# Block sums loaded one tile at a time, the last attention head's trip read ahead of other transfers, and three output tiles inside the steps

## The chip, the cores and the metric

The kernel runs on one core of a Trainium2 chip. The metric is the time of one execution on the device, in microseconds (us). A core has a matrix engine (TensorE, PE in the profile), a vector engine (VectorE, DVE), a scalar engine (ScalarE, ACT), a general engine (GpSimd, POOL) and a sync engine (SyncE, SP) that here does nothing but issue transfers (DMAs). ACT and POOL issue transfers too. Each engine works through its own list of instructions in order, and stops at an instruction whose operands aren't ready. So whatever stands behind a waiting transfer in SP's list waits with it, though it may itself be ready.

## The reference

One transformer block on 512 tokens and 16 meta tokens, model width 1024, in f32: half a feed-forward network (FFN), a mixer, and half of a second FFN.

```
h = h + 0.5 * swiglu(rmsnorm(h, ffn1_norm), ffn1_w_gate, ffn1_w_up, ffn1_w_down)     # width 2816
u = rmsnorm(h, mix_norm)
rq, rk, rv, rg, aq, ak, av, iq, ik, iw, g_ret, g_att = split(u @ w_in)
yr = (silu(rg) * retention(rq, rk, rv)) @ w_ret_out          # 4 heads, keys 256 wide, values 512 wide
ya = sparse_attention(aq, ak, av, iq, ik, iw) @ w_att_out    # 8 heads of 128; the keys of a query
                                                             # are picked by an indexer
h = h + (sigmoid(g_ret) * yr + sigmoid(g_att) * ya) @ w_mix_out
h = h + 0.5 * swiglu(rmsnorm(h, ffn2_norm), ffn2_w_gate, ffn2_w_up, ffn2_w_down)
y = rmsnorm(h, final_norm)[:, 16:]
```

## The kernel before

**Products.** An f32 product is made of three matmuls. Each operand is split into a high part and a low remainder, and `mm3` issues high by high, high by low, low by high for every 128 rows k of the contraction (line 170). For a weight tile, ACT copies `raw` into `whi` (the high part) and DVE subtracts to get `wlo` (the low one). Of the three matmuls of a k, the third needs `wlo`.

**Steps.** The mixer is written as a list of steps, run by `steps_through`: each has a tile of weights (loaded into `raw` by SP, four steps ahead), its split (two steps ahead), and its matmuls. In steps marked "dma" DVE is spared (`in_two_by_dma`): ACT writes the high part into `whi` (line 310) and its negative into `wlo` (line 311), and POOL issues a transfer that adds `raw` onto `wlo` (line 312). That transfer has to land before the step's third matmul. PE, ACT and DVE run in the order in which the program is written. SP and POOL are ordered by a scheduler, except for transfers that are kept in program order (`tc.keep_in_program_order`).

**Block sums.** The second FFN uses sums and differences of blocks of its weights. `block_sums(8)` forms those of `w_down` early, beside the last 37 retention steps: for each of 8 indices k, four tiles `wq` (256 KB each) are loaded by SP (line 1578), DVE makes four sums in place (line 1590), and four stores put them into DRAM as `wx` (line 1582). `with_block` hooks one piece of this to the end of each step. Most of those 37 steps are products of retention: gates, queries, keys, and the four output products of each head, `outputs(p)`. Those of the last head, `outputs(3)`, have the PE tile `psro`; the step after them is a gate (`psgate`). All five are "dma" steps.

**Attention.** For head h, `half_scores(h)` makes the probabilities in tokens by keys, and `trip(h)` writes them to DRAM (`pt`, issued by POOL, line 2279; even and odd heads have a `pt` of their own). `fetch(h)` reads them back the other way round (`turned`, SP, line 2292). `come_back` splits them into `pth` (ACT) and `ptl` (DVE). `weigh_v(h)` multiplies them with the values (`psao`), and its result is split into `vo` high (ACT) and low (DVE): the parts `ao_parts[h]`. A gate made between (`gate_product`, `psga`) is written to DRAM as `gd` (line 2356). The product with `w_att_out` needs all 8 heads' parts, one k for each head. Two of its eight output tiles (`psat`) are begun inside the steps, by `out_step`, with k = 0 to 6; the last head's `weigh_v` comes after them, and `out_tile_ends` adds k = 7.

Of the kernel before, what the change touches and what calls it, by code (L numbers as in the profile page):

```python
# [18 lines left out]
P = 128  # L19
D = 1024  # L20
KD = D // P
S = 512
# [11 lines left out]
AH = 8  # L34
# [47 lines left out]
def kernel(ctx: ExitStack, tc: tile.TileContext, x, meta, g1, wg1, wu1, wd1, gm,  # L82
                      w_in, w_ro, w_ao, w_mo, g2, wg2, wu2, wd2, gf, rope, decay, causal, out):
    nc = tc.nc
# [42 lines left out]
    w_at = [8]  # L127


    raw_room, raw_at = [], [0]  # L130

    def four_rooms():

# [3 lines left out]
    def load_w(src, nk, n):  # L137
        if raw_room:
            both = nk * n > 1024
            at = (raw_at[0] + (both and raw_at[0] % 2)) % 4  # L140
            raw_at[0] = at + 1 + both
            raw = raw_room[at // 2][:, at % 2 * 1024 :]
        else:
            raw = wpool.tile([P, 2048], F32, tag="raw", name="raw", bufs=2)
        v = raw[:, : nk * n].rearrange("p (k c) -> p k c", k=nk)
        nc.sync.dma_start(v, src.rearrange("(k p) c -> p k c", p=P))
        return v

    def split_w(v, eng=nc.vector):
# [208 lines left out]
    class Sevens:  # L358
# [97 lines left out]
        def catch_up(self):  # L456

            now, self.behind = self.behind, []
            for do in now:
                do()  # L460
# [1103 lines left out]
    def block_room(tag):  # L1564
        if tag == "R":
            return cpool.tile([P, T], F32, tag="R", name="wq", bufs=2)[:, :S]
        if tag == "ssum2":
            return cpool.tile([P, T], F32, tag="ssum2", name="wq")[:, :S]
        return bp.tile([P, S], F32, tag=tag, name="wq")

    def block_sums(n):

        def bring(k):

            ts = []
            for tag, (half, cs) in zip(("R", "R", "ssum2", "caus"), BLOCKS):
                ts.append(block_room(tag))
                tc.keep_in_program_order(nc.sync.dma_start(ts[-1], wrows[half][:, k, cs]))
            return ts

        def store(i, k):
            tc.keep_in_program_order(nc.sync.dma_start(wx[i, :, k, :], ts[BLOCK_SUMS[i][0]]))

        ts = bring(0)
        yield
        for k in range(n):
            for i, (to, x, y, op) in enumerate(BLOCK_SUMS):
                if i:
                    store(i - 1, k)
                nc.vector.tensor_tensor(ts[to], ts[x], ts[y], op)  # L1590
                if k % 2 == 0 or i != 2:
                    yield
            store(3, k)
            if k + 1 < n:
                ts = bring(k + 1)
                yield

    accs, vrs = ExitStack(), ExitStack()
    acc_r = []
# [33 lines left out]
    if True:  # L1633
# [438 lines left out]
        def with_block(step):  # L2072

            def run(w, lower):
                step[2](w, lower)
                next(block_steps, None)
            return (*step[:2], run, *step[3:])
# [41 lines left out]
        def attention_steps(kind, what, tiles_):  # L2119

            def step(i, t):
                return (t[0], lambda: in_parts(t[1]()), lambda w, lower: at_step[kind](*what, i, w, lower), 0)
            return [step(i, t) for i, t in enumerate(tiles_)]
# [7 lines left out]
        for h in range(AH):  # L2131
# [5 lines left out]
            else:  # L2137
                more += gate_for("scored gate", h)
            more += gate_for("weighed gate", h)
        more += attention_steps("out", (), tiles(w_ao, 0, 2))  # L2140
        steps[-37:] = [with_block(step) for step in steps[-37:]]
        last_step = steps[-1]
        steps[-1] = (*last_step[:2], lambda w, lower: (last_step[2](w, lower), at_step.update(begun=True)), *last_step[3:])
        steps += more
# [48 lines left out]


    vrs.close()
    ao_cols, psats = Cols(w_ao, 0, KD), []
    def out_tile_ends(w, ps):

        mm3([(ps, slice(0, S))], [part[:, KD - 1 :] for part in w], lambda k: ao_parts[KD - 1], 1, False, True, True)
        return ps  # L2200

    with pool("ao") as ao:
        vo = [ao.tile([P, AH, S], F32R, tag=f"vo{i}", name="vo") for i in range(2)]
        ao_parts = [(vo[0][:, c, :], vo[1][:, c, :]) for c in range(AH)]
        with pool("at") as at:
# [139 lines left out]
            def gate_product(kind, c, w, place):  # L2345

                ps = place()
                mm3([(ps, REAL)], w, xs, KD)

                def taken():  # L2350
                    t = at.tile([P, S], F32, tag="gate", name="gate", bufs=2)
                    tanh_half(t, ps)
                    if kind == "gr":
                        pending.append(lambda: gate_twice(c, t))
                    else:
                        nc.sync.dma_start(gd[KD + c], t)
                return taken

            def wide_place():
# [106 lines left out]

            def out_step(i, w, lower):

                catch_up()
                ps = sm_tile("psat") if i else mm_tile("psat")[:, :S]  # L2470
                mm3([(ps, slice(0, S))], w, lambda k: ao_parts[k], KD - 1, onto=True)
                psats.append((w, ps))
                lower()
                lower()
                for low in come_back(((0, 1), (2, 3))[i]):
                    low()

# [4 lines left out]
            with tc.manual_schedule(engines=BUSY):  # L2482
                for _ in pipe:
                    pass
                weigh_v(AH - 1)()()
            ao_cols.next_at(2)

        mgs = ExitStack()
        mgp = mgs.enter_context(pool("mgp", 1, side="right"))
        mg = []  # L2490
        with pool("ou") as ou:
            tp.update(pool=ou, bufs=3)
            for c in range(2):
                t = ou.tile([P, S], F32, tag="gate", name="gate", bufs=1)
                nc.scalar.dma_start(t, gd[c])
                gate_acc(c, t)
            psats = [out_tile_ends(*a) for a in psats]
            for c in range(KD):
                if c < len(psats):
                    ps = psats[c]  # L2500
                else:
                    w = ao_cols.next()
                    ps = sm_tile("psat")
                    mm3([(ps, slice(0, S))], w, lambda k: ao_parts[k], KD)
                t = ou.tile([P, S], F32, tag="sa", name="sa", bufs=3)
                nc.scalar.dma_start(t, gd[KD + c])
                nc.vector.scalar_tensor_tensor(t, t, 1.0, ps, ALU.add, ALU.mult)
                if c in doubled:
                    nc.vector.tensor_tensor(t, t, acc_r[c], ALU.add)
                else:  # L2510
                    nc.vector.scalar_tensor_tensor(t, t, 0.5, acc_r[c], ALU.mult, ALU.add)
                mh = mgp.tile([P, S], F32R, tag=f"mh{c}", name="mh")
                ml = mgp.tile([P, S], F32R, tag=f"ml{c}", name="ml")
                if c in doubled:
                    nc.scalar.activation(mh, t, AF.Copy, scale=0.5)
                    nc.vector.scalar_tensor_tensor(ml, t, 0.5, mh.bitcast(F32), ALU.mult, ALU.subtract)
                else:
                    split(t, mh, ml)
                mg.append((mh, ml))
# [8 lines left out]
    with pool("om") as ou:  # L2528
        tp.update(pool=ou, bufs=3)
        def to_tokens(c, hc):  # L2530
            ps = sm_tile("psht")
            for b in range(4):
                nc.tensor.transpose(ps[:, b * P : (b + 1) * P], hc[:, b * P : (b + 1) * P], ident)
            for b in range(4):
                nc.scalar.activation(hTok[b][:, c * P : (c + 1) * P], ps[:, b * P : (b + 1) * P], AF.Copy)

        cols = Cols(w_mo, 0, KD)
        pend = None
        for c in range(KD):
            hc = ou.tile([P, S], F32, tag="hc", name="hc", bufs=4)  # L2540
            nc.scalar.dma_start(hc, hd[c])
            w = cols.next()
            ps = sm_tile("psmo")
            mm3([(ps, slice(0, S))], w, lambda k: mg[k], KD)
            if pend:
                to_tokens(*pend)
            nc.vector.tensor_tensor(hc, ps, hc, ALU.add)
            h, l = new_x(c)
            if c % 4 == 0:
                s2.new_scaled()  # L2550
            xc = s2.xn[c // 4][:, c % 4, :]
            nc.scalar.activation(xc, hc, AF.Identity, scale=gains[:, 2, c : c + 1])
            split(xc, h[:, :S], l[:, :S])
            add_square(hc, ssum3, c == 0, ou, S)
            pend = (c, hc)
        last_tokens = lambda a=pend: to_tokens(*a)
        RS = slice(0, S)


        norm = rstd_steps(ssum3, S, D, R3, ou, lambda: sm_tile("psn"))  # L2560
        raw_room.clear()
        raw0 = load_w(wg2[:, 0 : 2 * P], KD, 2 * P)
        ps0 = [sm_tile("psg") for _ in range(2)]
        for i in range(2):
            w = split_w(raw0[:, :, i * P : (i + 1) * P])
            mm3([(ps0[i], RS)], w, xs, KD)
            if i == 0:
                last_tokens()
                next(norm)
        raw0 = load_w(wu2[:, 0 : 2 * P], KD, 2 * P)  # L2570
        w = split_w(raw0[:, :, :P])
        for _ in norm:
            pass
# [369 lines left out]
```

## Time and profile before

| | |
|---|---|
| median of 3 runs | 1502.78 us (1502.63 to 1506.17) |
| the profiled execution's own time | 1504.8 us |
| its span in the profile | 1503.0 us |
| mean granted clock of PE | 0.996 of full speed |
| transfers | 283.65 MB, mean 189 GB/s |
| block sums beside the steps | 32 loads, 32 sums, 32 stores of 128x512 |

The views used below: the page has the busy time of each engine. The waits list, by engine and instruction, how long an engine stood idle until what released it ("engine line waited for: us in total, times, longest us"). A timeline has one row for an instruction: its start in us from the span's start, its duration, the engine (PE, ACT, DVE, POOL; with a q, as SPq, the queue in which it issues transfers), line, operation, tiles, and in brackets the idle time before it with what ended it. For a transfer the duration is that of the issue, not of the move. Windows give, for a stretch of time A:B, its length, the busy time of PE, PE's weight loads, DVE, ACT and POOL with their counts, the granted clock of PE (1.00 is full speed), the transfer engines' share of time, and GB/s. The chain of waits is the path that ended last in a stretch, with start and length of each piece; there a transfer has its whole time to landing.

### The profile page before, as it was taken

To read this page: it belongs to the slowest core of one execution; us is meant where nothing else is said; L and a number is where in the kernel's file an instruction comes from. 1 tells how busy PE (TensorE), PEld (TensorE's weight loads), DVE (VectorE), ACT (ScalarE), POOL (GpSimd) and SP (SyncE) were. 2 spreads that over 40 slices of the span, in tenths; PEclk is the share of its full clock that TensorE was granted. 3 is DMA by queue.
4 is the path that set the end of the run, shared out by engine and by line. 5 is a ranking of instruction groups with operands and counts; after the bars stand their busy time and mean duration, and the time that the engine had idled before them with its cause. 6 is when DMAs were issued, how large, how long until landed. Compare 5 with 4: busy or idle time off the path is not lost.

```text
span 1503.0 us, 24593 instructions
## 1 busy us (share of the span) xinstructions
PE 1486.1 (99%) x9535; PEld 1339.2 (89%) x9535; DVE 1175.5 (78%) x1781; ACT 779.6 (52%) x1248; POOL 223.4 (15%) x311
## 2 busy tenths in 40 slices
PE   9999999999999999999999989999999999999998
PEld 8999999999888888788798878889788889999986
DVE  4999999788887767677968676778565779998878
ACT  5655555466354444544334436766445445555555
POOL 1012221001110121102010012111102003322101
PEclk9999999999999999999999999999999999999999
DMA  5259898886553455578685597676653224455693
GB/s 177 85 179 270 259 282 260 265 292 220 182 190 141 155 165 140 129 213 190 171 248 158 163 256 189 187 211 176 210 172 110 84 85 135 155 174 175 236 322 137
DMA packets 206102, 283.65 MB, mean 189 GB/s; under 512 B 10976, under 2 KB 138104, under 8 KB 205088
## 3 DMA queue, kind: packets, MB, share of 16 engines
q1 hardware_dynamic: 170992, 213.71, 43.9%
q0 software_dynamic: 31600, 62.52, 16.9%
q10 hardware_dynamic: 3392, 5.84, 1.1%
q8 instruction: 75, 1.23, 0.3%
q14 instruction: 43, 0.35, 0.1%
HBM read 212.79 MB, written 60.31 MB: 182 GB/s over the span
## 4 chain that ended last, share of the span: by engine, by line
PE 87%; DVE 5%; DMA 3%; issue 3%; ACT 1%; POOL 0%; POOLq 0%; ACTq 0%; SPq 0%; DVEq 0%
PE psqX L170 12%; PE psrg L170 6%; PE psqY L170 5%; PE psvX L1365 4%; PE psro L170 4%; PE psga L170 3%; PE psrk L170 3%; PE psu L170 3%; PE psrq L170 3%; PE psmo L170 3%; PE psqZ L170 3%; PE psaq L170 3%; PE psX L1040 2%; PE psak L170 2%; PE psat L170 2%
## 5 line engine op out<-in xcount | busy, mean ns | idle before, releaser
L305 ACT ACTIVATE whi<-raw 128x1024 fp32r<-128x1024 f32 (+2 forms) x216 | 204.1, 946 | 137.0 <-PE psqZ L170 21.2
L306 DVE TENSOR_TENSOR wlo<-raw,whi 128x1024 fp32r<-128x1024 f32 (+2 forms) x216 | 237.8, 1102 | 42.9 <-ACT whi L305 41.9
L170 PE MATMUL psqX<-th,whi 128*128 128x264 f32 (+1 forms) x432 | 123.3, 285 | 1.3 <-DVE g L552 0.9
L170 PE MATMUL psqX<-tl,whi 128*128 128x264 f32 (+1 forms) x432 | 122.2, 283 | 0.0
L170 PE MATMUL psqX<-th,wlo 128*128 128x264 f32 (+1 forms) x432 | 122.2, 283 | 0.0
L305 ACT ACTIVATE whi<-wsum 128x1024 fp32r<-128x1024 f32 x72 | 76.1, 1057 | 40.2 <-issue 21.3
L306 DVE TENSOR_TENSOR wlo<-wsum,whi 128x1024 fp32r<-128x1024 f32 x72 | 86.6, 1217 | 0.7 <-ACT whi L305 0.6
L170 PEld LDWEIGHTS psqX<-th,whi 128*128 128x128 f32 x432 | 82.0, 190 | 2.4 <-DVE g L552 1.1
L170 PEld LDWEIGHTS psqX<-tl,whi 128*128 128x128 f32 x432 | 82.0, 190 | 0.0
L170 PEld LDWEIGHTS psqX<-th,wlo 128*128 128x128 f32 x432 | 82.0, 190 | 0.0
L170 PE MATMUL psro<-vo,whi 128*128 128x512 f32 x256 | 81.3, 399 | 0.5 <-DVE accr L2008 0.5
L312 POOL DMA_DIRECT2D wlo<-raw x21 | 28.4, 1354 | 252.0 <-ACT wlo L311 96.2
L170 PEld LDWEIGHTS psro<-vo,whi 128*128 128x128 f32 x256 | 49.4, 193 | 11.7 <-ACT whi L310 0.9
L170 PE MATMUL psro<-vo,wlo 128*128 128x512 f32 x128 | 51.6, 403 | 4.3 <-DMA wlo<-raw 4.3
L117 ACT ACTIVATE whi<-raw 128x1024 fp32r<-128x1024 f32 (+1 forms) x31 | 31.8, 1028 | 41.5 <-PE psmo L170 21.2
L170 PE MATMUL psrg<-xh,whi 128*128 128x512 f32 x128 | 51.8, 405 | 0.0
L170 PE MATMUL psrg<-xh,wlo 128*128 128x512 f32 x128 | 50.0, 390 | 0.0
L170 PE MATMUL psrg<-xl,whi 128*128 128x512 f32 x128 | 49.9, 390 | 0.0
L2731 POOL TENSOR_TENSOR ts<-g 128x256 f32<-128x256 f32 x16 | 22.3, 1412 | 176.6 <-DVE g L563 176.6
L306 DVE TENSOR_TENSOR wlo<-w,whi 128x1024 fp32r<-128x1024 f32 x30 | 36.5, 1222 | 13.1 <-ACT whi L305 13.1
L118 DVE TENSOR_TENSOR wlo<-raw,whi 128x1024 fp32r<-128x1024 f32 (+1 forms) x31 | 36.8, 1187 | 8.2 <-ACT whi L117 8.1
L305 ACT ACTIVATE whi<-w 128x1024 fp32r<-128x1024 f32 x30 | 31.7, 1057 | 20.1 <-PE psvX L1365 10.9
(523 smaller groups left out, 4915.1 us busy)
## 6 DMA issues: line engine op xcount, KB each, us to landing
raw<-in_ffn_w_up_dram SPq DMA_DIRECT2D x22, 1024.0 KB, 5.9
raw<-in_ffn_w_gate_dram SPq DMA_DIRECT2D x21, 1024.0 KB, 6.9
raw<-in_w_in_dram SPq DMA_DIRECT2D x35, 512.0 KB, 4.7
raw<-in_ffn_w_down_dram SPq DMA_DIRECT2D x34, 512.0 KB, 4.6
raw<-in_w_in_dram SPq DMA_DIRECT2D x17, 1024.0 KB, 5.5
raw<-wx SPq DMA_DIRECT2D x32, 512.0 KB, 5.9
w<-in_w_in_dram SPq DMA_DIRECT2D x24, 512.0 KB, 6.2
wlo<-raw POOLq DMA_DIRECT2D x21, 512.0 KB, 5.7
```

Source lines behind the costliest of these rows:

```text
L117: nc.scalar.activation(hi, src, AF.Copy)
L118: eng.tensor_tensor(lo, src, hi.bitcast(F32), ALU.subtract)
L170: nc.tensor.matmul(o, a[:, k, :], b[:, sl], start=first and k == 0 and i == 0, stop=last and k == nk - 1 and i == 2, skip_group_check=onto)
L305: nc.scalar.activation(hi, src, AF.Copy)
L306: return lambda: nc.vector.tensor_tensor(lo, src, hi.bitcast(F32), ALU.subtract)
L312: return lambda: nc.gpsimd.dma_start(lo, src, accum_op=ALU.add)
L1040: nc.tensor.matmul(pss[c], a[:, k, c * P : (c + 1) * P], m[:, k, :], start=first and k == 0 and i == 0, stop=last and k == 1 and i == 2, s ...
L1365: nc.tensor.matmul(d[bank_][t], a, b[:, k, :], start=not onto and j + k + m == 0, stop=j + k == 3 and m == 2, skip_group_check=onto)
L2731: nc.gpsimd.tensor_tensor(ts[:, i], a, b, ALU.subtract)
```

## The change

Three edits. `block_sums` keeps four tiles for good; each is loaded again singly, when its sum has been stored, where four were loaded together before. It is hooked to `steps[-37:-3]`, so it ends three steps earlier. In attention, the transfers `gd` of the last two gates are issued by ACT instead of SP, and the `w_att_out` tiles that are loaded behind the steps are kept in program order (`raw_pinned`), which puts them behind the last head's `turned`. And three output tiles instead of two stand in the steps: two do k = 0 to 5, then comes the last head's `weigh_v`, then k = 6 of both, k = 7 of both, and the third tile whole.

```diff
-        nc.sync.dma_start(v, src.rearrange("(k p) c -> p k c", p=P))
+        ins = nc.sync.dma_start(v, src.rearrange("(k p) c -> p k c", p=P))
+        if raw_pinned:
+            tc.keep_in_program_order(ins)
         return v
...
-        def bring(k):
-
-            ts = []
-            for tag, (half, cs) in zip(("R", "R", "ssum2", "caus"), BLOCKS):
-                ts.append(block_room(tag))
-                tc.keep_in_program_order(nc.sync.dma_start(ts[-1], wrows[half][:, k, cs]))
-            return ts
+        ts = [block_room(tag) for tag in ("R", "R", "ssum2", "caus")]
+
+        def bring(j, k):
+            if k < n:
+                half, cs = BLOCKS[j]
+                tc.keep_in_program_order(nc.sync.dma_start(ts[j], wrows[half][:, k, cs]))
 
         def store(i, k):
-            tc.keep_in_program_order(nc.sync.dma_start(wx[i, :, k, :], ts[BLOCK_SUMS[i][0]]))
-
-        ts = bring(0)
+            if k >= 0:
+                tc.keep_in_program_order(nc.sync.dma_start(wx[i, :, k, :], ts[BLOCK_SUMS[i][0]]))
+
+        for j in range(4):
+            bring(j, 0)
         yield
         for k in range(n):
             for i, (to, x, y, op) in enumerate(BLOCK_SUMS):
-                if i:
-                    store(i - 1, k)
+                store((i - 1) % 4, k - (i == 0))
+                for j in {0: (0, 3) if k else (), 1: (), 2: (2,), 3: (1,)}[i]:
+                    bring(j, k + (i > 0))
                 nc.vector.tensor_tensor(ts[to], ts[x], ts[y], op)
-                if k % 2 == 0 or i != 2:
-                    yield
-            store(3, k)
-            if k + 1 < n:
-                ts = bring(k + 1)
                 yield
+        store(3, n - 1)
...
-        more += attention_steps("out", (), tiles(w_ao, 0, 2))
-        steps[-37:] = [with_block(step) for step in steps[-37:]]
+        more += attention_steps("out", (), tiles(w_ao, 0, 3))
+        steps[-37:-3] = [with_block(step) for step in steps[-37:-3]]
...
-    ao_cols, psats = Cols(w_ao, 0, KD), []
+    ao_cols, psats = Cols(w_ao, 3 * P, KD - 3), []
...
-                        nc.sync.dma_start(gd[KD + c], t)
+                        (nc.scalar if c >= KD - 2 else nc.sync).dma_start(gd[KD + c], t)
...
             def out_step(i, w, lower):
 
+                if i == 2:
+                    out_ = weigh_v(AH - 1)
+                    for a in psats:
+                        out_tile_goes_on(*a, KD - 2)
+                    out_()()
+                    for a in psats:
+                        out_tile_goes_on(*a, KD - 1)
+                    ps = sm_tile("psat")
+                    mm3([(ps, slice(0, S))], w, lambda k: ao_parts[k], KD)
+                    psats.append((w, ps))
+                    return
                 catch_up()
                 ps = sm_tile("psat") if i else mm_tile("psat")[:, :S]
-                mm3([(ps, slice(0, S))], w, lambda k: ao_parts[k], KD - 1, onto=True)
+                mm3([(ps, slice(0, S))], w, lambda k: ao_parts[k], KD - 2, onto=True)
                 psats.append((w, ps))
-                lower()
-                lower()
+                if i == 0:
+                    lower()
+                    lower()
                 for low in come_back(((0, 1), (2, 3))[i]):
                     low()
...
-                weigh_v(AH - 1)()()
-            ao_cols.next_at(2)
-
...
+                    raw_pinned[:] = [True]
                     w = ao_cols.next()
```

`out_tile_goes_on(w, ps, k)` takes the place of `out_tile_ends`: the three matmuls of one k onto a tile. In the changed kernel a line has a number larger by 2 (lines 170, 1578, 1582) or smaller by 1 (lines 2292, 2356).

The first place is SP's list around `outputs(3)`; the `w_ret_out` loads of 128x4x512 are the weights of that head's four products, `w_in` those of the steps behind. Before:

```order
L1582 DMA wx<-wq 128x512 x3
L1578 DMA wq<-in_ffn_w_down_dram 128x512 x4
L146 DMA raw<-in_w_ret_out_dram 128x4x512
L1582 DMA wx<-wq 128x512
L146 DMA raw<-in_w_ret_out_dram 128x4x512
L1582 DMA wx<-wq 128x512 x2
L146 DMA raw<-in_w_in_dram 128x8x128 x2
L1582 DMA wx<-wq 128x512
L1578 DMA wq<-in_ffn_w_down_dram 128x512 x4
L146 DMA raw<-in_w_in_dram 128x8x128 x2
L1582 DMA wx<-wq 128x512
```

In the changed kernel, from the same two `w_ret_out` loads on:

```order
L146 DMA raw<-in_w_ret_out_dram 128x4x512
L1580 DMA wq<-in_ffn_w_down_dram 128x512
L1584 DMA wx<-wq 128x512
L1580 DMA wq<-in_ffn_w_down_dram 128x512
L1584 DMA wx<-wq 128x512
L1580 DMA wq<-in_ffn_w_down_dram 128x512
L146 DMA raw<-in_w_ret_out_dram 128x4x512
L1580 DMA wq<-in_ffn_w_down_dram 128x512
L1584 DMA wx<-wq 128x512 x2
L146 DMA raw<-in_w_in_dram 128x8x128 x2
L1584 DMA wx<-wq 128x512 x2
L146 DMA raw<-in_w_in_dram 128x8x128 x9
```

The four last loads of `wq`, which stood together behind the first two `w_in` loads and a store, now stand singly among the stores, ahead of those two `w_in` loads; behind them only two stores are left.

The second place is SP's list at the end of attention (`pt_89` is the DRAM tile of even heads, `pt_90` that of odd ones; the last head is odd). Before:

```order
L2356 DMA gd<-gate 128x512
L2292 DMA turned<-pt_89 128x512 x4
L146 DMA raw<-in_w_att_out_dram 128x8x256
L2356 DMA gd<-gate 128x512 x2
L146 DMA raw<-in_w_att_out_dram 128x8x256
L2292 DMA turned<-pt_90 128x512 x4
L146 DMA raw<-in_w_att_out_dram 128x8x256
```

In the changed kernel:

```order
L2355 DMA gd<-gate 128x512
L2291 DMA turned<-pt_89 128x512 x4
L2291 DMA turned<-pt_90 128x512 x4
L146 DMA raw<-in_w_att_out_dram 128x8x256 x2
L146 DMA raw<-in_w_att_out_dram 128x8x128
```

Two `gd` stores and two loads of weights no longer stand between the last two heads' reads.

The third place is PE's list right behind the last head's `weigh_v`, whose last matmul is the first row; `vo_9495` and `vo_9496` (`vo_9467` and `vo_9468` in the changed kernel) hold the high and low parts of all heads, and each `psat` number is one output tile. Before:

```order
L1760 MATMUL psao_11391<-ptail_9504,vtail_9502 128x16
L170 MATMUL psat_11328<-vo_9495,whi_11166 128x512
L170 MATMUL psat_11328<-vo_9496,whi_11166 128x512
L170 MATMUL psat_11328<-vo_9495,wlo_11167 128x512
L170 MATMUL psat_11358<-vo_9495,whi_11269 128x512
L170 MATMUL psat_11358<-vo_9496,whi_11269 128x512
L170 MATMUL psat_11358<-vo_9495,wlo_11270 128x512
L170 MATMUL psat_11448<-vo_9495,whi_11444 128x512
```

In the changed kernel:

```order
L1760 MATMUL psao_11362<-ptail_9476,vtail_9474 128x16
L172 MATMUL psat_11303<-vo_9467,whi_11139 128x512
L172 MATMUL psat_11303<-vo_9468,whi_11139 128x512
L172 MATMUL psat_11303<-vo_9467,wlo_11140 128x512
L172 MATMUL psat_11332<-vo_9467,whi_11242 128x512
L172 MATMUL psat_11332<-vo_9468,whi_11242 128x512
L172 MATMUL psat_11332<-vo_9467,wlo_11243 128x512
L172 MATMUL psat_11303<-vo_9467,whi_11139 128x512
L172 MATMUL psat_11303<-vo_9468,whi_11139 128x512
L172 MATMUL psat_11303<-vo_9467,wlo_11140 128x512
L172 MATMUL psat_11332<-vo_9467,whi_11242 128x512
```

The six matmuls right behind `weigh_v` were those of k = 7, which use its result; now six of k = 6, which don't, stand between. The number of matmuls is the same.

More of the change, by code (lines that the diff above doesn't have):

```diff
@@ L127 @@
     w_at = [8]
-    raw_room, raw_at = [], [0]
+    raw_room, raw_at, raw_pinned = [], [0], []
     def four_rooms():
@@ L2195, with out_tile_goes_on @@
     vrs.close()
-    ao_cols, psats = Cols(w_ao, 0, KD), []
-    def out_tile_ends(w, ps):
-        mm3([(ps, slice(0, S))], [part[:, KD - 1 :] for part in w], lambda k: ao_parts[KD - 1], 1, False, True, True)
-        return ps
+    ao_cols, psats = Cols(w_ao, 3 * P, KD - 3), []
+    def out_tile_goes_on(w, ps, k):
+        mm3([(ps, slice(0, S))], [part[:, k:] for part in w], lambda _: ao_parts[k], 1, False, True, True)
     with pool("ao") as ao:
@@ L2496 @@
                 gate_acc(c, t)
-            psats = [out_tile_ends(*a) for a in psats]
             for c in range(KD):
                 if c < len(psats):
-                    ps = psats[c]
+                    ps = psats[c][1]
                 else:
+                    raw_pinned[:] = [True]
                     w = ao_cols.next()
@@ L2535, in to_tokens @@
                 nc.scalar.activation(hTok[b][:, c * P : (c + 1) * P], ps[:, b * P : (b + 1) * P], AF.Copy)
+        raw_pinned.clear()
         cols = Cols(w_mo, 0, KD)
```

## The prediction

> **What bounds the kernel.** I read the page first, then PE's waits, then the timeline and windows at the longest waits.
>
> ```profile
> span 1503.0 us, 24593 instructions
> PE 1486.1 (99%) x9535; PEld 1339.2 (89%) x9535; DVE 1175.5 (78%) x1781; ACT 779.6 (52%) x1248; POOL 223.4 (15%) x311
> ```
>
> PE is busy for 99% of the span, and the change takes no matmul away. So it can gain only what PE loses by standing idle, 16.9 us in all, or by a lower clock. The waits say where PE stands idle:
>
> ```profile
> PE psro L170 <- DMA wlo<-raw: 4.3, 1, 4.3
> PE psrq L170 <- DMA wlo<-raw: 0.7, 1, 0.7
> PE psat L170 <- ACT vo L305: 0.7, 1, 0.7
> PE psao L1759 <- ACT pth L305: 0.5, 1, 0.5
> PE psro L170 <- DVE accr L2008: 0.5, 1, 0.5
> ```
>
> The largest is a single wait, in `outputs(3)`. PE's timeline has the first row of each of its four products, and the row at which it stood:
>
> ```profile
> 859.33 0.63 PE L170 MATMUL psro<-vo,whi 128*128 128x512 f32 x2
> ...
> 864.84 0.62 PE L170 MATMUL psro<-vo,whi 128*128 128x512 f32 x2
> ...
> 870.33 0.62 PE L170 MATMUL psro<-vo,whi 128*128 128x512 f32 x2
> 875.29 0.80 PE L170 MATMUL psro<-vo,wlo 128*128 128x512 f32 x1 [4.34 <-DMA wlo<-raw]
> ...
> 883.23 0.62 PE L170 MATMUL psro<-vo,whi 128*128 128x512 f32 x2
> ```
>
> Products 0 and 1 take 5.51 and 5.49 us. Product 2 takes 883.23 - 870.33 = 12.90. It loses 7.4 us, though PE waited only 4.34. The other 3.1 are in the clock:
>
> ```profile
> 874.00:875.00 1.00, 0.00 (x0) 0.00 (x0) 1.00 (x3) 0.00 (x0) 0.32 (x1) 0.75 1.26 204
> 881.00:882.00 1.00, 1.00 (x5) 0.85 (x4) 0.00 (x0) 0.00 (x0) 0.00 (x0) 0.84 1.13 333
> ```
>
> The seventh column is the granted clock. A mean of 0.75 from 874 to 875 is a fall to half speed at about 874.5, some 3.6 us after PE's last matmul; 0.84 from 881 to 882 is a return at about 881.3. So this one late transfer costs more than twice its wait. The Trainium skill, "TensorE: Matmul & The Clock Gate", Part 1, has half rate after an idle window of about 3.4 us, full rate again after about as long of sustained work, and calls the length variable between runs. The fall agrees; the return took nearly twice as long here, from 875.29 to 881.3.
>
> **Part one: single loads of the block sums.** What made the transfer late? Rows of ACT, SP and POOL, and its piece of the chain of waits:
>
> ```profile
> 864.29 1.04 ACT L311 ACTIVATE wlo<-raw 128x1024 fp32r<-128x1024 f32 x1
> 864.79 0.34 SPq L1582 DMA_DIRECT2D wx<-wq  x1
> 865.18 3.07 SPq L1578 DMA_DIRECT2D wq<-in_ffn_w_down_dram  x4
> 865.63 1.27 POOL L312 DMA_DIRECT2D wlo<-raw  x1 [8.79 <-ACT wlo L311]
> 865.63 9.61 DMA wlo<-raw
> 865.63:875.24 9.61, 5.32 (x24) 4.03 (x22) 8.77 (x18) 5.35 (x7) 3.42 (x3) 0.96 1.11 235
> ```
>
> The low part's transfer left at 865.63 and landed 9.61 us later. The four `wq` loads left from 865.18 to 868.25, beside it. The two transfers of the same kind before it, in the stretch 848 to 857, had landed sooner, with no `wq` load beside them:
>
> ```profile
> DMA to landing us min/median/max: 5.1/5.1/5.1
> ```
>
> In the changed order the last `wq` load stands ahead of the `w_in` loads that were issued before 864.79, so nothing of the burst is left beside this transfer. In its 9.61 us, 9.61 x 235 GB/s = 2.26 MB moved; the burst is four times 128x512x4 bytes, 1.05 MB. At the same rate the rest takes 4.5 us less, so landing comes at 870.8. Up to one store more than before (0.26 MB) falls into the stretch: 1.1 us by the same rate. I take half of that, 871.3. PE needs the data at 870.33 + 2 x 0.23 = 870.8 (three matmuls take 0.69, as 5.5/8). So 0.5 us of waiting remains, too short to lower the clock: the wait of 0.5 us for `accr` lies in a stretch at 1.00 (730 to 740, below). Gain 7.4 - 0.5 = 6.9. Ends: 7.4 when it lands in time, by the row of 5.1 us; 5.5 when it lands at 872.7, halfway between that row's 870.7 and 874.7.
>
> ACT's copy into `wlo`, which ends at 865.33, sets when the transfer leaves; the change leaves it as it is. Of the sums themselves, equally many remain: 32 loads, 32 stores, and 32 of
>
> ```profile
> L1590 DVE TENSOR_TENSOR wq<-wq x32: 680/684/693, 650.7 to 890.2; 128x512 f32<-128x512 f32 x32
> ```
>
> Each load now waits in SP's list for the store ahead of it, and that for a sum on DVE. Behind it wait the loads of weights, which are issued four steps of 5.5 us ahead and land in 4.4 to 5.5 us by the page; a wait of one step costs nothing.
>
> The same collision is behind PE's second wait:
>
> ```profile
> 736.91 2.42 SPq L1578 DMA_DIRECT2D wq<-in_ffn_w_down_dram  x4
> 736.42 10.03 DMA wlo<-raw
> 746.50 0.50 PE L170 MATMUL psrq<-xh,wlo 128*128 128x512 f32 x1 [0.71 <-DMA wlo<-raw]
> ```
>
> With single loads the transfer lands some microseconds earlier: gain 0.7, all of the wait (0 if two or three single loads fall beside it all the same). Against this stands DVE, which has no time to spare just there:
>
> ```profile
> 730.00:740.00 10.00, 9.50 (x42) 7.53 (x41) 9.90 (x20) 4.43 (x5) 3.10 (x2) 1.00 0.64 184
> ```
>
> PE's 0.5 us for `accr` is a wait for this full DVE. As the sums now run in fewer steps, up to two more may be ahead of that `accr`; each is 0.68. Ends: nothing, and 1.2 lost. I take 0.2, near the lower end, since total work there is unchanged and only its phase moves.
>
> **Part two: the end of attention.** Rows of POOL, ACT, SP, PE and DVE:
>
> ```profile
> 1058.57 2.58 POOL L2279 DMA_DIRECT2D pt<-turned  x4 [18.01 <-DVE turned L2273]
> ...
> pt<-turned POOLq DMA_DIRECT2D x4, 256.0 KB, 4.6
> ...
> 1065.42 1.75 SPq L2356 DMA_DIRECT2D gd<-gate  x2
> ...
> 1068.19 2.43 SPq L2292 DMA_DIRECT2D turned<-pt  x4
> ...
> 1073.72 2.30 ACT L305 ACTIVATE pth<-turned 128x512 fp32r<-128x512 f32 x4 [5.95 <-DMA turned<-pt]
> 1074.40 0.50 PE L1759 MATMUL psao<-pth,vo 128*128 128x512 f32 x1 [0.51 <-ACT pth L305]
> 1075.12 0.50 PE L1759 MATMUL psao<-ptl,vo 128*128 128x512 f32 x1 [0.23 <-DVE ptl L306]
> ...
> 1077.21 0.60 ACT L305 ACTIVATE vo<-psao 128x512 fp32r<-128x512 f32 x1 [0.85 <-PE psao L1760]
> 1077.87 0.49 PE L170 MATMUL psat<-vo,whi 128*128 128x512 f32 x1 [0.71 <-ACT vo L305]
> 1078.59 0.50 PE L170 MATMUL psat<-vo,whi 128*128 128x512 f32 x1 [0.23 <-DVE vo L306]
> ```
>
> The last head's `pt` is in DRAM by 1058.57 + 2.58 + 4.6 = 1065.7 at the latest. The read of it leaves only at 1068.19, since in SP's list it stands behind two `gd` and a load of weights. Without these it can leave at 1065.7, land at about 1071, and `pth` follows 2.5 us earlier. PE comes to `weigh_v` 1.37 us earlier (six matmuls of 0.23 fewer ahead), so the waits of 0.51 and 0.23 both vanish. The six matmuls of k = 6 take the same 1.37 us, and the split of `vo` from 1077.21 until DVE ends, 0.64 + 0.69 later, takes 1.33: the other two waits vanish too. Sum 0.51 + 0.23 + 0.71 + 0.23 = 1.68, and the starts of those matmuls are further apart by 0.8 more; I take 2.0. Ends: 2.5, and 0.2 when the read gains nothing and the matmuls moved behind `weigh_v` bring its wait forward. For the two `gd`, ACT pays two issues; its row for one such issue:
>
> ```profile
> 1077.28 0.36 ACTq L2495 DMA_DIRECT2D gate<-gd  x1
> ```
>
> That is 0.7 us on an engine that stood idle for 5.95 ahead of `pth`: nothing. The Trainium skill, "DMA: Bandwidth & Descriptors", section "Issuing engines are not separate DMA queues", says that transfers from several engines run on the same 16 engines, so that issuing elsewhere saves only the issue. By that the two `gd` would bring 1.75 us of SP's time and no bandwidth; what counts in the rows is the place behind an unready transfer, which it doesn't speak of. The third tile's 24 matmuls are the same ones as before, their weights split two steps ahead: nothing.
>
> **Sum.** -6.9 - 0.7 + 0.2 - 2.0 = -9.4 us. On the profiled execution that makes 1504.8 - 9.4 = 1495.4, on the median, 2.0 below it, 1493.4. I predict 1494 for the median. The best ends, 7.4 + 0.7 + 0 + 2.5 = 10.6, give 1492.2; the worst, 5.5 + 0 - 1.2 + 0.2 = 4.5, give 1498.3. A measurement of this kernel tells some 0.3%, 4.5 us, from no change.
>
> **Rivals.** First: the transfer in `outputs(3)` stays late, because it isn't the burst's size that delays it but sharing with anything at all: two `wx` stores, later loads of `w_in`, and the next transfer of its kind, which POOL issues 1.9 us after it. If it lands after about 874.2, PE still idles over 3.4 us and the clock still falls; part one gives about nothing there, part two and `psrq` 2.7, so 1500.1. For it speaks that
>
> ```profile
> DMA to landing us min/median/max: 4.4/5.7/12.1
> ```
>
> over the 17 such transfers from 635 to 880 spread widely; against it, that the two long ones looked at both had a burst beside them. In the Trainium skill, "DMA: Bandwidth & Descriptors", section "Queues, rings and completion order", each transfer engine goes round the queues that have work, a packet from each. By that, what counts is whether SP's queue has work during the transfer, not how much stands in it; then two stores would slow it by their own time alone. Chance 0.13.
>
> Second, slower: the loads that no longer come in bursts come beside a low part's transfer that was undisturbed. The nearest are those of the gates, in POOL's rows:
>
> ```profile
> 698.71 1.60 POOL L312 DMA_DIRECT2D wlo<-raw  x1 [1.70 <-ACT wlo L311]
> 705.13 1.59 POOL L312 DMA_DIRECT2D wlo<-raw  x1 [3.71 <-DMA wlo<-raw]
> ```
>
> The second was issued only when the first had landed (the wait of 3.71), 6.4 us after it left. None of PE's longer waits is there, so the margins hold as they are; with some 4 us of further delay and more PE would idle long enough to lose the clock, at 7.4 a time. Two such places lose 14.8 against gains of 9.4: 1508.2. One of them gives 1500.8, still within 0.3%. Chance 0.06 for the loss.
>
> **Chances.** Forecast 0.81, within 1492.2 to 1498.3; still late 0.13; slower 0.06. So faster by over 0.3% 0.81, within 0.3% 0.13, slower 0.06. The range runs from 1491.5 (the best ends and 0.7 for scatter of the runs) to 1500, which takes in most of the first rival.
>
> **What would show it.** In the changed profile: the third product of `outputs(3)` takes 5.5 to 6 us, the granted clock stays at 1.00 from 870 to 885, PE's wait for `wlo` there is under 1 us; the `turned` read of the last head leaves about 2.5 us sooner after POOL's `pt`; the four waits at `psao` and `psat` are gone; PE's idle time is about 9 instead of 16.9 us. It is wrong if a `psro` or `psrg` wait over 3.4 us with a clock of 0.5 stands anywhere, or if a new wait stands at `psat` for `whi` or `wlo` of the third tile.

## The result

| kernel | median, us | runs | ratio to before, 95% interval |
|---|---|---|---|
| before | 1502.70 | 4 | |
| changed | 1494.38 | 4 (1493.16 to 1495.18) | 0.9940 [0.9928, 0.9952] |
| changed, once more | 1493.87 | 5 | 0.9936 [0.9922, 0.9949] |

The changed kernel is faster by 8.3 us, and by 9.5 in the second comparison, whose runs of before had a median of 1503.32. 1494 was forecast. Between the two profiled executions, 1504.8 and 1494.25, the difference is 10.55; the profiled run of before lay 2.1 above the median of its kernel, that of the changed kernel at it.

The changed kernel's page, and PE's waits in it:

```profile
span 1492.5 us, 24589 instructions
PE 1481.5 (99%) x9535; PEld 1336.6 (90%) x9535; DVE 1175.1 (79%) x1781; ACT 779.9 (52%) x1248; POOL 223.0 (15%) x311
```

```profile
PE psqX L172 <- DVE g L554: 1.5, 1, 1.5
PE psg L655 <- DVE idle L623: 1.5, 1, 1.5
PE psro L172 <- DVE accr L2008: 0.8, 1, 0.8
PE psn L1811 <- DVE tmp L308: 0.3, 1, 0.3
PE psat L172 <- DVE wlo L118: 0.2, 1, 0.2
```

No wait of PE's matmuls for a `wlo` transfer is left, nor one for `pth`, `ptl` or `vo`. PE's idle time is 1492.5 - 1481.5 = 11.0 us, against 16.9 before; 6.4 of it lie behind its last matmul, and 6.5 did before. PE's busy time fell too, by 4.6 us, though it does the same 9535 matmuls: at half clock a matmul counts as busy for longer (0.80 us in the prediction's row at 875.29, 0.50 for its like at 746.50 at full clock). PE's timeline has the first row of each of the four products of `outputs(3)`, and two windows the clock there (seventh column):

```profile
858.74 0.63 PE L172 MATMUL psro<-vo,whi 128*128 128x512 f32 x2
...
864.25 0.62 PE L172 MATMUL psro<-vo,whi 128*128 128x512 f32 x2
...
869.75 0.62 PE L172 MATMUL psro<-vo,whi 128*128 128x512 f32 x2
...
875.33 0.62 PE L172 MATMUL psro<-vo,whi 128*128 128x512 f32 x2
```

```profile
860.00:870.00 10.00, 10.00 (x46) 8.17 (x44) 8.85 (x18) 5.78 (x8) 2.54 (x2) 1.00 0.84 199
870.00:880.00 10.00, 10.00 (x45) 8.09 (x44) 9.76 (x24) 3.61 (x4) 0.87 (x1) 1.00 0.97 198
```

The third product takes 5.58 us instead of 12.90, at full clock. Its low part's transfer, by POOL's line from 863 to 866:

```profile
L314 POOL DMA_DIRECT2D wlo<-raw x1: 1271/1271/1271, 865.1 to 865.1; - x1
...
  PEld psro L172: 0.2, 1
...
DMA to landing us min/median/max: 5.1/5.1/5.1
```

It landed in 5.1 us instead of 9.6, just in time: only PE's weight load had to wait, for 0.2 us.

Where the time went shows in the starts of three stages, by tile (the last two numbers are the first and last start). Before, then changed:

```profile
L170 PE MATMUL psat<-vo,whi x128: 389/389/499, 1064.1 to 1112.1; 128*128 128x512 f32 x128
...
L170 PE MATMUL psmo<-mh,whi x64: 389/389/486, 1112.5 to 1158.3; 128*128 128x512 f32 x64
```

```profile
L172 PE MATMUL psat<-vo,whi x128: 387/389/477, 1056.2 to 1102.0; 128*128 128x512 f32 x128
...
L172 PE MATMUL psmo<-mh,whi x64: 389/389/486, 1102.5 to 1148.3; 128*128 128x512 f32 x64
```

The changed kernel is 0.6 us ahead at the first product of `outputs(3)` (859.33 against 858.74), 7.9 at the first output tile, 10.0 at the product after attention. So `outputs(3)` gave 7.3 us, the end of attention 2.1, and what lies ahead 0.6. In that 0.6 two things cancel that the change doesn't touch: 0.8 us gained in the first 8 us of the kernel, and 0.8 lost by 166 us, mostly in `psqX`. The last 0.5 came in the second FFN, which the change doesn't touch either.

### The profile page after: what moved, and what is told of

The parts are those of the page before. It is cut to its first block, busy times and chain, and to the rows that moved or that the text cites. A ratio compares the mean times of both kernels' runs of the same rounds, so it can differ in the third digit from the quotient of the medians.

```text
span 1492.5 us, 24589 instructions
## 1 busy us (share of the span) xinstructions
PE 1481.5 (99%) x9535; PEld 1336.6 (90%) x9535; DVE 1175.1 (79%) x1781; ACT 779.9 (52%) x1248; POOL 223.0 (15%) x311
## 4 chain that ended last, share of the span: by engine, by line
PE 89%; DVE 6%; DMA 2%; issue 2%; ACT 1%; POOL 0%; ACTq 0%; POOLq 0%; DVEq 0%
PE psqX L172 12%; PE psqY L172 6%; PE psrg L172 5%; PE psro L172 5%; PE psvX L1367 4%; PE psga L172 3%; PE psrk L172 3%; PE psu L172 3%; PE psqZ L172 3%; PE psrq L172 3%; PE psmo L172 3%; PE psaq L172 3%; PE psat L172 2%; PE psX L1042 2%; PE psak L172 2%; PE psg L172 2%
## 5 line engine op out<-in xcount | busy, mean ns | idle before, releaser
L307 ACT ACTIVATE whi<-w 128x1024 fp32r<-128x1024 f32 x30 | 31.7, 1057 | 20.1 <-PE psvX L1367 10.9
```

What stands on the lines that cost most here:

```text
L307: nc.scalar.activation(hi, src, AF.Copy)
```

## The experiments

All ratios are to runs of before on the same chip. Their medians were 1502.93 (experiments 1 to 4), 1502.58 (5 to 8) and 1503.32 (9 to 11).

### The parts alone

The first experiment is the changed kernel with the old block sums:

```diff
-        steps[-37:-3] = [with_block(step) for step in steps[-37:-3]]
+        steps[-37:] = [with_block(step) for step in steps[-37:]]    # and block_sums as before
```

> The changed kernel with the block sums of before (four loads together, 37 steps): only the end of attention is changed. Theory (the parts add up): the four waits of 0.51, 0.23, 0.71 and 0.23 us at psao and psat are gone, 2.0 us less, 1500.7 against 1502.7; the wait of 4.3 us in outputs(3) and the clock of 0.5 behind it stay. Rival (the late transfer is cured by something other than single loads, such as the shifted steps behind): the wait of 4.3 us shrinks here too, and the time is near 1495.

Measured: 1500.92 us, 0.9989 [0.9980, 0.9997], 2.0 less. The wait of 4.3 us for `wlo` in `outputs(3)` stands, and so do 0.7 at `psrq` and a clock of 0.73 from 870 to 880. The waits at `psao` and `psat` are gone.

The second is the kernel before with the new `block_sums` and its 34 steps, and nothing else.

> The kernel before with the single loads of the block sums alone. Theory: the low part's transfer for the third product of outputs(3) lands in about 5.1 us, PE doesn't wait there, the clock stays at 1.00; 7.4 + 0.8 us less by the profile, so some 1495 to 1496.5; the four waits at psao and psat stay. Rival (single loads only move the collision to other low parts): a new wait for wlo of 1 us or more stands elsewhere, and the time is above 1498.

Measured: 1496.31 us, 0.9957 [0.9944, 0.9969], 6.6 less. In the profile no wait is left in `outputs(3)` or at `psrq`. One wait for a low part that the profile of before doesn't list stands at a gate, 0.4 us at `psrg`. It can't be put down to the single loads: 0.2 to 0.5 us stand there also in experiments 1, 3, 4 and 9, which have the four loads together. The two parts alone make 8.6 us, the whole 8.3 and 9.5: they add up, within the intervals.

### What made PE lose 7.4 us

The third experiment leaves the four loads together and the kernel as before, but takes the one transfer away:

```diff
-            return steps_of(tiles(w_ro[h * DV : (h + 1) * DV, :], 0, 4, DV // P, 2 * P),
+            made = steps_of(tiles(w_ro[h * DV : (h + 1) * DV, :], 0, 4, DV // P, 2 * P),
                             [step(i) for i in range(4)], *how)
+            if how:
+                made[2] = made[2][:4]        # no "dma": DVE makes this wlo
+            return made
```

> The kernel before, with the burst of four loads left where it is; only the weights of the third product of outputs(3) are split by DVE (1.2 us) instead of by ACT and a transfer. Theory (PE lost 7.4 us there because that one transfer was late): the third product takes about 5.5 us, the clock stays at 1.00, and the time falls by 7.4 less what DVE's 1.2 us costs, to 1495.3 to 1496.5. Rival (the burst slows something else too, such as raw loads or stores that DVE's sums wait for): the next low part or accr is late instead, with a wait of 2 us or more, and the time stays above 1499.

Measured: 1496.30 us, 0.9958 [0.9945, 0.9970], 6.6 less, as much as all of the single loads brought. DVE's row of the low part, and the windows:

```profile
864.39 1.22 DVE L306 TENSOR_TENSOR wlo<-raw,whi 128x1024 fp32r<-128x1024 f32 x1
```

```profile
860.00:870.00 10.00, 10.00 (x45) 8.23 (x44) 8.67 (x17) 5.23 (x7) 1.27 (x1) 1.00 0.83 230
870.00:880.00 10.00, 10.00 (x45) 8.19 (x44) 9.86 (x21) 3.60 (x4) 0.87 (x1) 1.00 0.84 173
```

PE is busy throughout, at full clock, with the burst in its old place. So this burst cost time only through this transfer; the wait of 0.7 us at `psrq`, beside an earlier burst, is still there.

The next two put bytes back beside it, in the changed kernel: two more loads of 128x512, and these with two more stores.

```diff
+                if k == n - 1 and i == 3:
+                    for j in (1, 2):
+                        half, cs = BLOCKS[j]
+                        tc.keep_in_program_order(nc.sync.dma_start(ts[j], wrows[half][:, k, cs]))
+                    for j in range(2):       # the sixth experiment alone
+                        tc.keep_in_program_order(nc.sync.dma_start(more_wx[j], ts[0]))
                 nc.vector.tensor_tensor(ts[to], ts[x], ts[y], op)
```

> The changed kernel with two more loads of 128x512 (0.52 MB in all, into tiles that are no longer used) in SP's list right behind the store that leaves just ahead of the low part's transfer of outputs(3)'s third product. Theory (the transfer is late by the bytes beside it): before, 1.05 MB beside it cost 9.61 - 5.07 = 4.5 us, so 0.52 MB cost 2.3: it lands 7.3 us after it leaves, PE waits about 2.1 us, too short for the clock to fall; some 1496.5. Rival (what counts is that SP's queue has work at all, not how much): it is as late as before, with a wait over 4 us and the clock at half; some 1502.

> The same with two loads and two stores of 128x512 more (1.05 MB, as in the burst of before; the stores go to a place that nothing reads). Theory: the transfer lands some 9.6 us after it leaves, PE waits about 4.4 us, the clock falls to half for some 6 us, and the third product takes 12.9 us again; 7.4 us more than the changed kernel, 1501.8. So twice the bytes cost more than three times the time of two. Rival (the late transfer of before came from where the burst stood in the sums, not from its bytes): no such wait, below 1496.

Measured: 1496.72 us with two (0.9961 [0.9946, 0.9976]) and 1500.15 with four (0.9986 [0.9977, 0.9995]), 2.3 and 5.8 above the changed kernel. Of each, the transfer in the chain of waits, PE's row after it, and the window. With two:

```profile
863.53 7.00 DMA wlo<-raw
...
870.57 0.50 PE L172 MATMUL psro<-vo,wlo 128*128 128x512 f32 x1 [1.74 <-DMA wlo<-raw]
...
870.00:880.00 10.00, 9.43 (x41) 7.77 (x42) 8.43 (x20) 2.10 (x3) 0.87 (x1) 1.00 1.08 245
```

With four, with two later rows of PE and one window more:

```profile
865.20 9.21 DMA wlo<-raw
...
874.45 0.79 PE L172 MATMUL psro<-vo,wlo 128*128 128x512 f32 x1 [3.94 <-DMA wlo<-raw]
...
878.46 0.63 PE L172 MATMUL psro<-vo,wlo 128*128 128x512 f32 x1
...
879.74 0.39 PE L172 MATMUL psro<-vo,wlo 128*128 128x512 f32 x1
...
870.00:880.00 10.00, 6.06 (x17) 4.43 (x16) 6.42 (x16) 2.54 (x3) 0.87 (x1) 0.66 1.09 226
872.00:873.00 1.00, 0.00 (x0) 0.00 (x0) 1.00 (x3) 0.72 (x1) 0.00 (x0) 0.96 1.16 276
```

The landing goes with the bytes: 5.1, 7.0 and 9.2 us with 0, 0.52 and 1.05 MB added, about 1.0 us for each 256 KB. So the rival by which any traffic is as bad as a burst is out. With the wait of 1.74 us the clock stays at 1.00; in that of 3.94 it falls, and PE's matmuls of 0.63 us become ones of 0.39 again only between 878.46 and 879.74. A mean of 0.96 from 872 to 873 is a fall at 872.9, 2.4 us after PE fell idle (874.45 - 3.94 = 870.51), where 3.6 had passed in the profile of before. The record of the granted clock has 6.8 us at half in both profiles; PE ran in 6.0 of them before and in 5.3 here. The expected time with four was 1501.8, so the cost of 7.4 came out as 5.8.

### The end of attention

The fourth experiment is the kernel before, with the read placed early (the `gd` stores by ACT, the later loads in program order) and its two output tiles as they were.

> The kernel before with the last head's read ahead of the gate stores and of the loads of w_att_out, and two output tiles as before (k = 0 to 6 ahead of weigh_v). Theory (two separate waits): the waits for pth and ptl (0.51 + 0.23) go, those for vo (0.71 + 0.23) stay; 1.0 us less, 1501.7. Rival (one chain: an earlier read alone takes away all four): 2.0 us less. Second rival (the read is not what pth waits for): no gain.

Measured: 1508.33 us, 1.0040 [1.0026, 1.0054]. That is slower by 5.4 us, which no expectation had. The waits for `pth` and `ptl` went and those for `vo` stayed, as the theory said. But one that hadn't been there came; PE's waits, the window, and rows of ACT and POOL:

```profile
PE psat L172 <- ACT whi L117: 3.7, 1, 3.7
```

```profile
1075.00:1085.00 10.00, 5.82 (x16) 3.68 (x17) 5.43 (x8) 2.92 (x5) 3.04 (x2) 0.83 0.56 180
```

```profile
1079.61 0.33 ACTq L2498 DMA_DIRECT2D gate<-gd  x1
1079.98 1.06 ACT L117 ACTIVATE whi<-raw 128x1024 fp32r<-128x1024 f32 x1 [4.79 <-DVE sa L2510]
...
1078.32 1.26 POOL L1625 TENSOR_TENSOR accr<-accr,gate 128x512 f32<-128x512 f32 x1 [18.00 <-DMA gate<-gd]
```

The weights of the third output tile now come behind the read, so their split slid on ACT's list behind the second gate load. That load needs the tile that POOL's product frees at 1079.58, and `whi` waited with it: so the chain of waits goes, though the bracket in `whi`'s row names DVE. PE stood for 3.7 us, and the clock fell. The ninth experiment splits those weights right behind `vo`, and is otherwise the same:

```diff
                 weigh_v(AH - 1)()()
+                ao_cols.next_at(2)
+                raw_pinned[:] = [True]
+                early = [ao_cols.next()]
```

> The fourth experiment (early read, two output tiles as before), with the third tile's weights split right behind the last head's vo on ACT and DVE, instead of behind the two gate loads on ACT's list. Theory (the third tile's whi was late because ACT's second gate load stood ahead of it and waited for POOL's product, 1078.32 to 1079.58; the weights themselves were there at 1073.56): the wait of 3.7 us at psat falls to 0.5 or less, the clock doesn't fall there, and the time is 1501 to 1502.5. Rival (the weights were loaded too late): the wait stays over 2 us and the time over 1506.

Measured: 1502.06 us, 0.9989 [0.9980, 0.9998]. The wait for `whi` is gone, and the end of attention has only

```profile
PE psat L172 <- ACT vo L307: 0.7, 1, 0.7
...
PE psat L172 <- DVE vo L308: 0.2, 1, 0.2
```

So the fourth was slow by ACT's order and not by the load. The early read alone, with this mended, is worth 1.3 us (0.3 to 3.0 by the interval). What the matmuls placed behind `weigh_v` add can't be told from the times, but PE's waits tell it: the 0.9 us for `vo` that stand here are gone in the first experiment. In the changed kernel the third tile inside the steps keeps the early read from costing 5 us: its weights are loaded and split before. The first experiment, which has the tile, the new order of matmuls and the old block sums, is 7.4 us faster than the fourth; no run takes the tile alone away.

The seventh experiment is the changed kernel without the line that keeps the later loads in program order.

```diff
-                    raw_pinned[:] = [True]
```

> The changed kernel, with the loads of w_att_out behind the steps no longer kept in program order: two of them stand ahead of the last head's read in SP's list, and wait there for room that DVE frees. Theory (the read's place in SP's list carries the gain at the end of attention): the read leaves some 4 us later than in the changed kernel, PE, which comes to weigh_v at 1064.4, waits 3 us or more for pth, and the time is 3 to 7 us above the changed kernel, 1497.5 to 1501.5. Rival (the order of the matmuls carries the gain): within 1 us of 1494.4.

Measured: 1503.02 us, 1.0003 [0.9994, 1.0012], 8.6 above the changed kernel and more than expected. SP's queue, the read's piece in the chain of waits, PE's wait and the window:

```profile
1062.17 2.36 SPq L146 DMA_DIRECT2D raw<-in_w_att_out_dram  x2
```

```profile
1064.71 7.74 DMA turned<-pt
```

```profile
PE psao L1759 <- ACT pth L307: 6.7, 1, 6.7
```

```profile
1065.00:1075.00 10.00, 3.31 (x11) 2.09 (x10) 1.80 (x4) 2.31 (x6) 0.00 (x0) 0.69 0.79 283
```

Two loads of weights stand ahead of the read. The second waits until DVE frees a room (1064.13 in the chain), and the read leaves behind it: 1.8 us before PE comes to `weigh_v` (1066.53), where the changed kernel had 6.8 (1057.69 against 1064.44). The two loads, 1 MB each, then move beside it, and its four pieces land in 7.6 us by their median instead of 4.6. The expectation had the first delay, 4 us, but not the slower landing. PE idles for 6.7 us; the mean clock of this window is 0.69. The profiled execution was the slowest of the ten, 1505.95.

The eighth gives the `gd` stores of the last two gates back to SP.

```diff
-                        (nc.scalar if c >= KD - 2 else nc.sync).dma_start(gd[KD + c], t)
+                        nc.sync.dma_start(gd[KD + c], t)
```

> The changed kernel with the gd stores of the last two gates issued by SP again, ahead of the last head's read. Theory (a read behind a store that isn't ready waits with it): the second gate ends at 1059.4 by ACT's row, so the read leaves at about 1060 instead of 1057.7, the last pth comes some 2 us later, PE waits 0.3 to 1.5 us at psao: 1494.7 to 1496. Rival (only the issue time counts, 0.35 us a store): under 0.7 us more, no wait at psao.

Measured: 1495.68 us, 0.9957 [0.9940, 0.9973], 1.3 above the changed kernel, which the intervals don't tell apart.

```profile
1057.27 1.75 SPq L2355 DMA_DIRECT2D gd<-gate  x2
1059.58 1.79 SPq L2291 DMA_DIRECT2D turned<-pt  x4
...
1058.08 0.60 ACT L1604 ACTIVATE gate<-psga 128x512 f32<-128x512 f32 x1
```

The read left 1.9 us later, at 1059.58 instead of 1057.69, as the theory had it. SP's 1.75 us hold two issues of 0.32; between them it waited for the second gate, which ACT ended at 1058.68. But no wait came at `psao`; there the rival was right, for the read had that much to spare. In this profile 0.5 and 0.3 us of waiting for the next tile's `wlo` and `whi` stand at `psat`, where the changed kernel has 0.2.

### A try at more

The tenth run is the changed kernel again, beside the eleventh:

> The changed kernel once more, to have it beside the next one on one chip: 1494.4, ratio to before 0.9945.

The eleventh adds an earlier split of the fourth output tile's weights, and block sums hooked one step earlier.

```diff
-        steps[-37:-3] = [with_block(step) for step in steps[-37:-3]]
+        steps[-38:-4] = [with_block(step) for step in steps[-38:-4]]
...
+            raw_pinned[:] = [True]
+            with tc.manual_schedule(engines={mybir.EngineType.Activation}):
+                early = [ao_cols.next()]
```

> The changed kernel with its two remaining waits attacked: the fourth output tile's weights are split ahead of ACT's second gate load (0.2 us of waiting at psat), and the block sums are hooked to the steps one earlier (steps -38 to -5), which moves the sum that stands ahead of the late accr (0.8 us). Theory: up to 1.0 us less than the changed kernel, 1493.4 to 1494.4; all of PE's idle time in the changed kernel is 3.9 us past the start, so no edit of waits can bring more. Rival (the shift brings a single load beside a gate's low part): a wait for wlo of 0.5 us or more, and no gain or a loss of 1 us.

Measured: 1502.27 us against 1493.87 for the changed kernel. The early `ao_cols.next()` let two loads slip ahead of the last head's read again, as in the seventh experiment, and the wait is the same:

```profile
PE psao L1759 <- ACT pth L307: 6.8, 1, 6.8
PE psg L655 <- DVE idle L623: 1.5, 1, 1.5
PE psro L172 <- DVE accr L2008: 0.8, 1, 0.8
```

The wait for `accr` stayed at 0.8, so the shift by a step did nothing to it. Whether the earlier split is worth its 0.2 us was not measured apart.

## Why the prediction was right, and where it was not

- **The bound.** It was PE's idle time and its clock, as the views of before said. Of the 10.55 us between the profiled executions, 7.3 came from one late transfer. One sign was added up wrong: PE's idle time was to be about 9 us, but the prediction's own waits, 4.34 - 0.5 + 0.7 - 0.2 + 1.68 = 6.0 less than 16.9, leave 10.9, and 11.0 was measured.
- **The number.** That the median came within 0.4 us of 1494 is partly luck. The sum gave 1493.4, and 0.6 was added without a reason; the profile gained more than the sum, the first comparison of medians less (8.3), the second as much (9.5).
- **The transfer in `outputs(3)`.** The term was 6.9 us, the profile shows 7.3. The low part landed 5.1 us after it left, where 5.7 had been taken (871.3 - 865.63); the extra store beside it cost nothing that shows. The doses confirm the step from bytes to landing: 4.5 us for 1.05 MB was the estimate, 4.1 was measured. The third experiment shows that in `outputs(3)` the burst mattered only through this transfer. The lower end of the term was worked out from a landing at 874.7, which no row shows; with the 875.24 of the row it would have been 5.2 instead of 5.5, and nothing hangs on it.
- **The clock.** That a wait of 0.5 us doesn't lower it and one of some 4 us does held in every profile: not at 1.74, but at 3.67, 3.94 and 4.34. The Trainium skill, "TensorE: Matmul & The Clock Gate", Part 1, puts the idle window at about 3.4 us. These waits lie on either side of it, but the time from PE's last matmul to the fall was not 3.4: it was 3.6 before, 2.4 in the sixth experiment and 2.2 in the seventh. How long half rate lasted was 6.83 us in the profiles of before and of experiments 1, 4, 6, 9 and 11; that is twice the page's 3.4. It wasn't so in every execution. The mean clock of each of the 55 executions of before that ran beside the experiments is on record: 0.998 in 15, 0.996 or 0.997 in the others. Behind the last matmul the clock falls too, for 3.7 to 6.2 us in the profiles, and 0.998 leaves room for 7.5 us at half in all; so those 15 had a shorter fall in `outputs(3)` than 6.83 us, or none. Their mean is 1.1 us lower (0.7 to 1.3 on each of three chips). So this is a part of why the median gained less than the profile; the rest isn't separated from other scatter.
- **`psrq` and `accr`.** 0.7 gained and 0.2 lost were forecast. The wait at `psrq` is gone, that for `accr` went from 0.5 to 0.8. Together the changed kernel was 0.6 ahead at that place, where 0.5 had been forecast.
- **The end of attention.** 2.0 was forecast, 2.1 is in the profile, 2.0 in the first experiment. The read's departure came out at 1065.7 by the working and at 1057.69 + 7.9 = 1065.6 by the profile, on the old time scale. The working was too kind in one point: it named the third output tile as costing nothing and saw no use in it. The fourth experiment shows its use. Without it, and with the old order of matmuls, the same early read loses 5.4 us, by a wait on ACT for which the prediction had no term. The prediction also read SP's 1.75 us for the two `gd` as time to issue them. Its row, like that of the eighth experiment, holds two issues of 0.32 us (at 1065.42 and 1066.85) and a wait between for the second gate, which ACT ended at 1066.82.
- **Gates by ACT.** The Trainium skill, "DMA: Bandwidth & Descriptors", section "Issuing engines are not separate DMA queues", says that issuing elsewhere saves only the issue. The eighth experiment doesn't contradict that: two issues of 0.32 us by SP are 0.64. But the read left 1.9 us later, mostly by the wait for the second gate, that is by its place behind a store that wasn't ready. The time rose by 1.3, which the intervals don't tell from nothing. In the seventh, where the place behind two loads was at stake, it rose by 8.6.
- **The rivals.** Sharing as such, 0.13: the doses speak against it. A collision moved elsewhere, 0.06: it isn't in the changed kernel's own two profiles. Of the variants with single loads, experiments 2, 5, 6 and 8 have 0.4 to 0.6 us at `psrg`, but four with the old block sums have 0.2 to 0.5 there too.

## What to carry to other kernels

Look first for a wait of several microseconds of PE, and price it with the clock's fall behind it: 4.3 us of waiting were worth 7.3 here. Waits of 3.67 us and more lowered the clock; nothing between 1.74 and 3.67 was measured. For a transfer that lands just in time, count the bytes that leave beside it, and move or split the bystanders before anything else. And when a read is moved ahead in an in-order list, follow what falls behind it to its next reader on every engine's list: here 2.0 us were gained with the new tile's weights split early, and 5.4 lost where a split had slid behind a waiting load.

## What the runs showed of the hardware that was not expected

A transfer's delay by its neighbours was close to proportional: 5.1, 7.0 and 9.2 us to landing with 0, 0.52 and 1.05 MB more beside 0.5 MB, loads and stores alike. And a wait of 3.94 us cost 5.8 us in the median, one of 1.74 cost 2.3: per microsecond of waiting the dearer one is not much dearer in the median, though in its profile PE's third product took 12.1 us (869.89 to 882.03) against 5.6.

The clock's fall didn't come at a fixed time after PE's last matmul, whose end the profile models. By the profiles' record of the granted clock, it fell 2.2 us after it in the seventh experiment, 2.4 in the sixth, 3.6 in the kernel before and 5.1 in the eleventh. It stayed at half for 3.41 us once (at `psat` in the fourth), for 6.83 in six profiles and for 10.24 once (in the seventh): always a whole multiple of 3.41. Since the fall can come 2.2 us into a wait, a wait not much longer than that may be enough; that wasn't measured.
